# Gate and up of the last feed-forward by seven block products in place of eight, on one Trainium2 core

## The chip, the cores and the metric

The kernel runs on one core of a Trainium2 chip, in one launch. The metric is the device time of one execution in microseconds (us), taken as the median of several executions. The engines go by their names in the profile: PE is TensorE (matrix products), DVE is VectorE, ACT is ScalarE, POOL is GpSimd, and SP is SyncE, which here only issues transfers. SBUF is the on-chip memory, and PSUM is the memory of eight banks into which PE accumulates.

## The reference

The reference is a two-layer block of a diffusion model, in fp32, with 512 latent tokens and 256 context tokens of 1024 features. Each layer mixes tokens in four ways, projects the mixed features (`w_out`), adds the residual, and runs a modulated SwiGLU feed-forward of inner width 2816. In the last layer only the latent tokens are needed. What matters here, cut from it:

```
def rms_norm(x, g):
    return x * lax.rsqrt(jnp.mean(x * x, axis=-1, keepdims=True) + NORM_EPS) * g

def swiglu(h, wg, wu, wd):
    return (jax.nn.silu(h @ wg) * (h @ wu)) @ wd

...
        x = x + g1 * (mix @ w_out[l])
        h = rms_norm(x, g_ffn[l]) * (1 + sc2) + sh2
        x = x + g2 * swiglu(h, w_gate[l], w_up[l], w_down[l])
```

## The kernel before

Features lie on the 128 partitions and tokens along the free axis, so x is eight tiles (`x`, one for each 128 features) of 128 x tokens. Every fp32 product is made of three matmuls (`mm3`, L63): operands are split into a high part in the reduced type fp32r and a rest, and PE multiplies high by high (L65), high by low (L66) and low by high (L67). Weights come in pieces of 128 x 512 (256 KB): SP loads one into a tile `raw` (`load_raw`, L69), ACT copies the high part into a tile `w` (L82), and DVE subtracts it to get the low part (L83). Layer 0 also lets POOL do a few of these.

The end of the last layer, where the change lies, has four stages:

1. Output projection: for each of eight tiles `mt`, 24 matmuls of 512 columns (`proj_out`). DVE adds the residual (L925, in `residual`), ACT squares x (L282) and DVE adds the squares up (L283, both in `Squares.add`), and ACT and DVE make the scaled and split tile `st` for the feed-forward (L253, L254, in `scaled`). The shift of the modulation rides along as two extra token columns.
2. Norm: four one-column matmuls sum the squares over the partitions (L292), DVE makes the reciprocal root (L100 to L109), four matmuls spread it over the partitions (L302), and ACT copies it (L304). The products gate and up need none of it: it is multiplied in afterwards.
3. Gate and up: for each of 22 column tiles `ft` of 128 features, 4 weight pieces and 2 x 2 x 8 groups of three matmuls of 256 or 258 columns. Each of the four results has a PSUM bank. DVE multiplies by the norm (L968, L970), ACT takes the Silu (L969), DVE multiplies the two (L971), and ACT and DVE split the result into a tile `h` (L92, L93).
4. Down: the 22 tiles are taken in three blocks of 8, 7 and 7 (`BLOCKS`). After each, eight output tiles are made from the block's `h` tiles with 512-column matmuls, and added to x.

Tiles share buffers by tag: `BUFS` gives eight to `h` and `st`, six to `w`, three each to `raw`, `T`, `pts` and `row`, two to `mraw`, four to `post`. A tile whose buffers are all in use waits until the oldest has been read for the last time. The order of the instructions on each engine is set when the program is built: a scheduler works it out from its own estimates of when each would be ready. On the chip each engine then goes through its list in that order, and SP through its loads, waiting where it must.

Of the kernel before, what the change touches and what calls it, by code (L numbers as in the profile page):

```python
# [9 lines left out]
F32R = mybir.dt.float32r  # L10
I32 = mybir.dt.int32
AF = mybir.ActivationFunctionType
OP = mybir.AluOpType
# [4 lines left out]
KT = 8  # L18
SEQ = 512
CTX = 256  # L20
NT = SEQ + CTX
DEPTH = 2
FFT = 22
BLOCKS = ((0, 8), (8, 15), (15, 22))
ORDER = (4, 6, 5, 7, 0, 2, 3, 1)

START = "s0 x1 x0 s1 w0 x2 x3 s2 x4 x5 s3 x6 x7 w1 s4 s5 s6 s7"
# [12 lines left out]
def hybrid_block(ctx: ExitStack, tc, t, out):  # L40
    nc = tc.nc
    V, S, G, T = nc.vector, nc.scalar, nc.gpsimd, nc.tensor
# [20 lines left out]
    def mm3(ps, ah, al, bh, bl, start, stop):  # L63

        T.matmul(ps, ah, bh, start=start, stop=False)  # L65
        T.matmul(ps, ah, bl, start=False, stop=False)  # L66
        T.matmul(ps, al, bh, start=False, stop=stop)  # L67
# [180 lines left out]
    def scaled(x, gain, sh, segs):  # L248

        hk = tile("st", [128, 2, NT + 2], F32R)  # L250
        for s0, s1, v in segs:
            hi, lo = [hk[:, z, s0 + 2 * v:s1 + 2 * v] for z in range(2)]
            last_s = S.activation(hi, x[:, s0:s1], AF.Copy, scale=gain[:, v:v + 1])  # L253
            last_v = V.scalar_tensor_tensor(lo, x[:, s0:s1], gain[:, v:v + 1], hi.bitcast(F32),  # L254
                                            op0=OP.mult, op1=OP.subtract)
        split_to(hk[:, 0, SEQ:SEQ + 2], hk[:, 1, SEQ:SEQ + 2], sh)
        made.append((last_s.ins, last_v.ins))
        return hk

    def scaled_proj(w, h, cuts, pss, k):  # L260
        for (c0, c1, *_), ps in zip(cuts[0], pss):
            mm3(ps[:, :c1 - c0], wf(w, k, 0), wf(w, k, 1), h[:, 0, c0:c1], h[:, 1, c0:c1], k == 0, k == KT - 1)

    def shift_of(cuts, pss):
        sh = small.tile([128, 2], F32, tag="sh", name="sh")
# [120 lines left out]
    for l in range(DEPTH):  # L386
        last = l == DEPTH - 1
        segs = segs_lat if last else segs_all
        ntok = segs[-1][1]
        m, a = mods[l]["m"], mods[l]["a"]  # L390
# [8 lines left out]
        first = [("win_c", 0), ("win_c", 1), ("win_dv", 0)]  # L399
        if l == 0:  # L400
# [3 lines left out]
            for what, k in START.split():  # L404
                k = int(k)
# [14 lines left out]
                if what + str(k) == "s5":  # L420
                    r = norm_spread(rr, segs_all, ("md", "md"))
            first = ws
            mods.append(new_mod(1))
        else:
            r = norm_spread(norm_scale(sq, segs_all), segs_all, ("tq", "md"))
            first = [feat_units(*x) for x in first]
# [16 lines left out]
        w = feat_units("win_dv", 1, "mraw")  # L443
# [487 lines left out]
        for mt in range(KT):  # L931
            w = wsplit(t["wout"][l, mt])
            outs = proj_out(w, KT, mh, ORDER, [[["pj", "pj", "tq", "md", "sc", "sc", "pt", "po"], ["pj", "pj", "tq", "md", "sc", "sc", "pt", "po"]][l][(mt * len(segs) + i) % 8] for i in range(len(segs))])
            x = xs[mt]
            residual(x, outs, per_feature(m, 2, mt))
            sq.add(x)
            sh = per_feature(m, 3, mt)
            h.append(scaled(x, a[:, 1, mt], sh[:, 0:1].to_broadcast([128, 2]) if last else sh, segs))

        turn[0] = 0  # L940
        r = norm_spread(norm_scale(sq, segs), segs, ("po", "pt"))
# [12 lines left out]
        work = steps()  # L954
        for b0, b1 in BLOCKS:
            hid = []
            for ft in range(b0, b1):
                gu = [wsplit(t["wg"][l, ft]), wsplit(t["wu"][l, ft])]
                gps, ups = [[psum_any() for _ in range(2)] for _ in range(2)]
                for w, pss in zip(gu, (gps, ups)):  # L960
                    for k in range(KT):
                        scaled_proj(w, h[k], cuts, pss, k)
                shg, shu = shift_of(cuts, gps), shift_of(cuts, ups)
                hd = tile("h", [128, 2, NT], F32R)
                for (_, _, s0, s1, v, o), g_, u_ in zip(cuts[0], gps, ups):
                    n = s1 - s0
                    sg, up = tile("post", [128, 512])[:, :n], tile("post", [128, 512])[:, :n]
                    V.tensor_mul(sg, g_[:, o:o + n], r[:, s0:s1])  # L968
                    S.activation(sg, sg, AF.Silu, bias=shg[:, v:v + 1])  # L969
                    V.tensor_mul(up, u_[:, o:o + n], r[:, s0:s1])  # L970
                    V.scalar_tensor_tensor(up, up, shu[:, v:v + 1], sg, op0=OP.add, op1=OP.mult)  # L971
                    split_to(hd[:, 0, s0:s1], hd[:, 1, s0:s1], up)
                for _ in range(3):
                    next(work, None)
# [62 lines left out]
def _layouts(i):  # L1037
    ac = np.ascontiguousarray
    L = DEPTH
    o = {}  # L1040
    xt = np.concatenate([i["x"][0].T, i["ctx"][0].T], 1)
    o["xt"] = ac(xt.reshape(KT, 128, NT).transpose(1, 0, 2))
    o["cc"] = ac(np.stack([i["c"][0], i["c_ctx"]], 1).reshape(KT, 128, 2).transpose(1, 0, 2))
    cols = []
    for u in range(2):
        cols += [np.arange(512) + 512 * u, np.arange(512) + 1024 + 512 * u]
    cols += [np.arange(2048, 6144)]
    cols = np.concatenate(cols)
# [24 lines left out]

    def featmajor(x, k):
        n = x.shape[2] // 128
        x = x.reshape(L, k, 128, n, 128).transpose(0, 3, 2, 1, 4)
        return ac(x)

    o["win_c"] = featmajor(i["w_in"][:, :, 1024:1280], KT).reshape(L, 2, 128, 1024)
    o["win_dv"] = featmajor(i["w_in"][:, :, 1792:2048], KT).reshape(L, 2, 128, 1024)  # L1080
    wo = np.concatenate([i["w_out"][:, swap], i["w_out"][:, 256:]], 1)
    o["wout"] = featmajor(wo, KT).reshape(L, KT, 128, 1024)
    o["wg"] = featmajor(i["w_gate"], KT).reshape(L, FFT, 128, 1024)
    o["wu"] = featmajor(i["w_up"], KT).reshape(L, FFT, 128, 1024)
    o["wd"] = featmajor(i["w_down"], FFT)
    for n in ("a_q_gain", "a_k_gain", "d_q_gain", "d_k_gain", "a_sink", "b_v_gain"):
        o[n] = ac(i[n])
    o["ws"] = ac(i["b_w_s"].transpose(0, 3, 1, 2).reshape(L, 128, 512))
    o["bs"] = ac(i["b_b_s"].transpose(0, 2, 1))

    o["wpool"] = ac(i["c_w_pool"].reshape(L, 2, 2, 64, 64).transpose(0, 2, 3, 1, 4))
    o["csc"] = ac(i["c_scale"].reshape(L, 2, 128).transpose(0, 2, 1))

    p = np.pad(i["d_rpb"], ((0, 0), (0, 0), (0, 0), (8, 9)))
    r, cq, kr, x = np.ogrid[:8, :16, :8, :32]
    o["rpb"] = ac(p[:, :, kr - r + 7, x - 8 - cq + 15 + 8].reshape(L, 4, 128, 8, 32))
    return o
# [17 lines left out]
```

## Time and profile before

| | |
|---|---|
| median of 3 runs | 1545.6 us (1543.95 to 1546.96) |
| the profiled execution | 1543.86 us |
| its span in the trace | 1542.1 us |
| mean granted TensorE clock in the span | 0.996 of full speed |
| PE busy | 1508.3 us (98%) |
| DVE busy | 956.9 us (62%) |
| ACT busy | 618.8 us (40%) |
| POOL busy | 118.3 us (8%) |

The span is the time from the first to the last instruction that the profile records; the execution's own time holds another 1.8 us. Busy time of an engine is the time in which at least one of its instructions runs. A matmul's recorded duration is longer than its share of PE's time, since matmuls overlap: what a matmul costs is the distance from its start to the start of the next.

### The profile page before, as it was taken

To read this page: it belongs to the slowest core of one execution; us is meant where nothing else is said; L and a number is where in the kernel's file an instruction comes from. 1 tells how busy PE (TensorE), PEld (TensorE's weight loads), DVE (VectorE), ACT (ScalarE), POOL (GpSimd) and SP (SyncE) were. 2 spreads that over 40 slices of the span, in tenths; PEclk is the share of its full clock that TensorE was granted. 3 is DMA by queue.
4 is the path that set the end of the run, shared out by engine and by line. 5 is a ranking of instruction groups with operands and counts; after the bars stand their busy time and mean duration, and the time that the engine had idled before them with its cause. 6 is when DMAs were issued, how large, how long until landed. Compare 5 with 4: busy or idle time off the path is not lost.

```text
span 1542.1 us, 26166 instructions
## 1 busy us (share of the span) xinstructions
PE 1508.3 (98%) x10098; PEld 1330.2 (86%) x10098; DVE 956.9 (62%) x2317; ACT 618.8 (40%) x1278; POOL 118.3 (8%) x107
## 2 busy tenths in 40 slices
PE   6899999999999999999999999899999999999999
PEld 4788787788888888888888888889889998998997
DVE  3789877686485624843375458899865443544453
ACT  5547655643322112221222344477654332332331
POOL 2521200100000000000000004542000000000000
PEclk9999999999999999999999999999999999999999
DMA  8443223342243313722273232201232233233223
GB/s 313 128 144 102 93 80 108 126 141 76 89 144 111 122 62 101 234 62 63 82 230 96 71 105 76 83 32 44 89 101 90 93 94 98 90 88 105 89 86 100
DMA packets 79324, 163.39 MB, mean 106 GB/s; under 512 B 12000, under 2 KB 17760, under 8 KB 79200
## 3 DMA queue, kind: packets, MB, share of 16 engines
q1 hardware_dynamic: 79200, 161.73, 32.8%
q8 instruction: 79, 1.29, 0.3%
q14 instruction: 45, 0.37, 0.1%
HBM read 157.50 MB, written 4.19 MB: 105 GB/s over the span
## 4 chain that ended last, share of the span: by engine, by line
PE 87%; DVE 6%; DMA 4%; ACT 2%; issue 1%; POOL 1%; SPq 0%; ACTq 0%; POOLq 0%
PE pj L65 9%; PE pj L66 9%; PE pj L67 9%; PE sc L66 6%; PE sc L65 6%; PE sc L67 6%; PE tq L65 3%; PE tq L66 3%; PE tq L67 3%; PE po L66 3%; PE po L65 3%; PE po L67 3%; PE po L350 2%; PE pt L66 2%; PE pt L65 2%; PE pt L67 2%
## 5 line engine op out<-in xcount | busy, mean ns | idle before, releaser
L82 ACT ACTIVATE w<-raw 128x512 fp32r<-128x512 f32 x368 | 227.1, 621 | 617.6 <-PE sc L67 154.2
L83 DVE TENSOR_TENSOR w<-raw,w 128x512 fp32r<-128x512 f32 x336 | 226.7, 677 | 242.9 <-ACT w L82 242.6
L65 PE MATMUL pj<-w,h 128*128 128x256 f32 x480 | 138.4, 289 | 6.7 <-DVE post L499 5.9
L66 PE MATMUL pj<-w,h 128*128 128x256 f32 x480 | 138.7, 289 | 0.0
L67 PE MATMUL pj<-w,h 128*128 128x256 f32 x480 | 137.7, 287 | 0.0
L65 PE MATMUL pj<-st,w 128*128 128x258 f32 (+2 forms) x384 | 120.4, 314 | 2.5 <-ACT st L253 2.3
L66 PE MATMUL pj<-st,w 128*128 128x258 f32 (+2 forms) x384 | 120.0, 313 | 0.0
L66 PE MATMUL sc<-st,w 128*128 128x258 f32 (+2 forms) x384 | 119.8, 312 | 0.0
L65 PE MATMUL sc<-st,w 128*128 128x258 f32 (+2 forms) x384 | 119.7, 312 | 0.0
L67 PE MATMUL pj<-st,w 128*128 128x258 f32 (+2 forms) x384 | 119.5, 312 | 0.0
L67 PE MATMUL sc<-st,w 128*128 128x258 f32 (+2 forms) x384 | 118.9, 310 | 0.0
L65 PEld LDWEIGHTS pj<-w,h 128*128 128x128 f32 x480 | 92.1, 192 | 13.9 <-ACT post L494 5.5
L83 POOL TENSOR_TENSOR w<-raw,w 128x512 fp32r<-128x512 f32 x32 | 43.0, 1354 | 739.0 <-DVE row L283 633.3
L66 PEld LDWEIGHTS pj<-w,h 128*128 128x128 f32 x480 | 92.4, 192 | 1.7 <-DVE post L499 0.8
L67 PEld LDWEIGHTS pj<-w,h 128*128 128x128 f32 x480 | 92.3, 192 | 0.3 <-issue 0.2
L65 PEld LDWEIGHTS pj<-st,w 128*128 128x128 f32 x384 | 73.1, 190 | 9.5 <-ACT st L253 3.5
L67 PEld LDWEIGHTS pj<-st,w 128*128 128x128 f32 x384 | 72.6, 189 | 5.5 <-issue 1.7
L65 PEld LDWEIGHTS sc<-st,w 128*128 128x128 f32 x384 | 73.2, 191 | 4.5
L66 PEld LDWEIGHTS pj<-st,w 128*128 128x128 f32 x384 | 72.7, 189 | 4.8 <-issue 0.4
L66 PEld LDWEIGHTS sc<-st,w 128*128 128x128 f32 x384 | 72.7, 189 | 4.2
L67 PEld LDWEIGHTS sc<-st,w 128*128 128x128 f32 x384 | 72.3, 189 | 4.0
L65 PE MATMUL po<-st,w 128*128 128x512 f32 (+1 forms) x192 | 66.2, 345 | 0.0
(308 smaller groups left out, 4117.9 us busy)
## 6 DMA issues: line engine op xcount, KB each, us to landing
mraw<-in_wmod SPq DMA_DIRECT2D x80, 512.0 KB, 3.9
raw<-in_wg SPq DMA_DIRECT2D x88, 256.0 KB, 2.5
raw<-in_wu SPq DMA_DIRECT2D x88, 256.0 KB, 2.6
raw<-in_wd SPq DMA_DIRECT2D x64, 256.0 KB, 2.7
h<-in_wslab SPq DMA_DIRECT2D x16, 512.0 KB, 8.1
raw<-in_wout SPq DMA_DIRECT2D x32, 256.0 KB, 2.6
x<-in_xt SPq DMA_DIRECT2D x16, 384.0 KB, 5.4
raw<-in_wd SPq DMA_DIRECT2D x32, 192.0 KB, 2.4
```

The lines of the kernel that those rows point to most:

```text
L65: T.matmul(ps, ah, bh, start=start, stop=False)
L66: T.matmul(ps, ah, bl, start=False, stop=False)
L67: T.matmul(ps, al, bh, start=False, stop=stop)
L82: S.activation(w[:, 0, :n], raw, AF.Copy)
L83: eng.tensor_sub(w[:, 1, :n], raw, w[:, 0, :n].bitcast(F32))
L350: T.matmul(o[64 * hh:64 * hh + 64, :128], vs[hh][lo:hi], pts[i, hh], start=i == 0, stop=i == n - 1)
```

## The change

In the last layer, gate and up are no longer made tile by tile. Two column tiles (`ft`, `ft + 1`) and the two halves of the tokens form a 2 x 2 block product over the two halves of the features (even and odd tiles of 128), and this is made from seven block products in place of eight (`strassen`). Each has 4 x 3 matmuls of 258 columns, and its operands are sums of blocks:

- `token_blocks` and `token_forms` make the seven token operands once for the whole stage, from each two tiles of x, in place of `scaled`: four blocks in a tile `mraw`, four sums in another (L291 to L294), and the split parts of all seven in the tiles `f1`, `f2`, `f3` (tags `T`, `bias` and `st`).
- `weight_forms` makes the seven weight operands of each pair and each of gate and up. Three are blocks of the weights as they are, two of them loaded as one tile `mraw` of 512 KB. The other four are sums, made by transfers: SP loads one block, and then POOL issues a second transfer that adds to it (`accum_op`, L313). Two of the sums, `s2` and `s4`, add a sum that was made before. All seven are then split as before, by ACT and DVE.
- The seven results in PSUM are put together by DVE (L347 to L356) and ACT (L346) into tiles `post`, and norm, Silu and the product of gate and up run over 512 tokens at a time.
- The blocks of the feed-forward are of 8, 8 and 6 column tiles in place of 8, 7 and 7, in both layers, and the weights of gate and up lie in another column order, which layer 0 follows by taking its slices in another order (`at`).

The diff, cut to its core:

```diff
-BLOCKS = ((0, 8), (8, 15), (15, 22))
+BLOCKS = ((0, 8), (8, 16), (16, 22))
...
+    def token_blocks(par, x, gain, sh, b):
+
+        S.activation(by128(b[:, 2 * par:2 * par + 2, 0:HN]), halves(x), AF.Copy, scale=gain[:, 0:1])
+        for h in (2 * par, 2 * par + 1):
+            V.tensor_copy(b[:, h, HN:HN + 2], sh[:, 0:1].to_broadcast([128, 2]))
+
+    def token_forms(b, single):
+
+        u = tile("mraw", [128, 4, HN + 2])
+        V.tensor_sub(u[:, 1], b[:, 0], b[:, 1])
+        V.scalar_tensor_tensor(u[:, 2], u[:, 1], -1.0, b[:, 3], op0=OP.mult, op1=OP.subtract)
+        V.tensor_add(u[:, 0], b[:, 2], u[:, 2])
+        V.tensor_sub(u[:, 3], b[:, 3], b[:, 1])
+        f1 = tile(single, [128, 1, 2, HN + 2], F32R)
+        f2 = tile("st", [128, 3, 2, HN + 2], F32R)
+        f3 = tile("st", [128, 3, 2, HN + 2], F32R)
+        for f, i, src in ((f2, 0, b[:, 2:4]), (f1, 0, b[:, 0:1]), (f3, 0, u[:, 1:4]), (f2, 2, u[:, 0:1])):
+            n = src.shape[1]
+            split_to(f[:, i:i + n, 0], f[:, i:i + n, 1], src)
...
+    def weight_forms(src):
+
+        both = load_raw(src[0], "mraw")
+        a11, a12 = both[:, 0:512], both[:, 512:1024]
+        a22 = load_raw(src[1][:, 512:1024], "raw", 512)
+
+        def plus(tag, first, more):
+
+            z = load_raw(first, tag, 512)
+            G.dma_start(z, more, accum_op=OP.add)
+            return z
...
+        s1 = plus("pts", src[1][:, 0:512], src[1][:, 512:1024])
+        s3 = plus("raw", src[0][:, 0:512], src[1][:, 0:512])
+        s2 = plus("pts", src[0][:, 0:512], s1)
+        s4 = plus("row", src[0][:, 512:1024], s2)
+        yield parts(a12)
+        yield parts(a11)
+        for x in (s1, s2, s4, a22, s3):
+            yield parts(x)
...
+        c1, c2 = tile("post", [128, 2, n]), tile("post", [128, 2, n])
+        u = tile("br", [128, n])
+        p2, p1 = product(2), product(1)
+        S.activation(u, p1, AF.Copy)
+        V.tensor_add(c1[:, 0], p2, u)
+        p5, p6 = product(5), product(6)
+        V.tensor_add(u, p6, u)
+        V.tensor_add(c1[:, 1], p5, u)
+        p3 = product(3)
+        V.tensor_add(c1[:, 1], p3, c1[:, 1])
+        p4, p7 = product(4), product(7)
+        V.tensor_add(c2[:, 0], p7, u)
+        V.scalar_tensor_tensor(c2[:, 1], p5, -1.0, c2[:, 0], op0=OP.mult, op1=OP.subtract)
+        V.tensor_sub(c2[:, 0], p4, c2[:, 0])
+        return c1, c2
...
+            for ft in range(b0, b1, 2) if last else ():
+                rv = halves(r)
+                gate = strassen([t["wg"][l, ft], t["wg"][l, ft + 1]], h)
+                for c in gate:
+                    cv = c[:, :, 0:HN]
+                    V.tensor_mul(by128(cv), by128(cv), rv)
+                    S.activation(cv, cv, AF.Silu, bias=c[:, 0, HN:HN + 1])
+                up = strassen([t["wu"][l, ft], t["wu"][l, ft + 1]], h)
+                for c, g_ in zip(up, gate):
+                    cv = c[:, :, 0:HN]
+                    V.tensor_mul(by128(cv), by128(cv), rv)
+                    V.scalar_tensor_tensor(cv, cv, c[:, 0, HN:HN + 1], g_[:, :, 0:HN], op0=OP.add, op1=OP.mult)
+                    hd = tile("h", [128, 2, NT], F32R)
+                    split_to(halves(hd[:, 0]), halves(hd[:, 1]), by128(cv))
+                    hid.append(hd)
```

The order of instructions moves in two places of which the prediction speaks. The first is on PE, where the last layer's output projection ends. The names are the results and operands: `po<-h,w` is the last output tile, `pj<-st,w` a gate product, `tq<-ones,row` the sum of squares and `po<-ident,ry` the spread of the norm. Before, the end of the projection is followed at once by gate products:

```order
L66 MATMUL po<-h,w 128x512
L67 MATMUL po<-h,w 128x512
L65 MATMUL pj<-st,w 128x256
L66 MATMUL pj<-st,w 128x256
L67 MATMUL pj<-st,w 128x256
L65 MATMUL pj<-st,w 128x258
```

and the sum of squares follows 41 gate matmuls after the last L67 of the projection:

```order
L65 MATMUL pj<-st,w 128x258
L66 MATMUL pj<-st,w 128x258
L292 MATMUL tq<-ones,row 128x1 x4
L67 MATMUL pj<-st,w 128x258
```

In the changed kernel the same place on PE reads so (L387 is what was L292, and L397 what was L302):

```order
L66 MATMUL po<-h,w 128x512
L67 MATMUL po<-h,w 128x512
L387 MATMUL tq<-ones,row 128x1 x4
L397 MATMUL po<-ident,ry 128x128 x4
L65 MATMUL pj<-st,w 128x258
L66 MATMUL pj<-st,w 128x258
L65 MATMUL pj<-T,w 128x258
L66 MATMUL pj<-T,w 128x258
```

The sum of squares and the spread of the norm now stand between the projection and the first product, with no other matmul beside them.

The second place is SP's list of loads from the last weights of the output projection (`in_wout`) on. Before, pieces of gate (`in_wg`) and up (`in_wu`) follow in turn, each into a `raw` tile:

```order
L72 DMA raw<-in_wout 128x512 x4
L72 DMA raw<-in_wg 128x512 x2
L72 DMA raw<-in_wu 128x512 x2
L72 DMA raw<-in_wg 128x512 x2
L72 DMA raw<-in_wu 128x512 x2
```

In the changed kernel (two loads into `pts` stand ahead of the last weights of the projection):

```order
L72 DMA raw<-in_wout 128x512 x4
L72 DMA raw<-in_wg 128x512 x2
L72 DMA raw<-in_wu 128x512
L72 DMA mraw<-in_wg 128x1024
L72 DMA mraw<-in_wu 128x1024
L72 DMA mraw<-in_wg 128x1024
L72 DMA row<-in_wg 128x512
L72 DMA pts<-in_wu 128x512
L72 DMA row<-in_wu 128x512
```

The tile `mraw` with the first two weight operands stands behind everything that held the two `mraw` buffers before, and the first load into `row` behind the third load into `mraw`. With it POOL, which had nothing to do in this stage, gets a list of transfers that add up. It starts so, with the tiles' numbers in the program: 12485 and 12491 are `s1` and `s2` of the first gate pair, 12488 its `s3`, 12494 its `s4`, and 12628, 12634 and 12637 are `s1`, `s2` and `s4` of the first up pair.

```order
L313 DMA pts_12485<-in_wg 128x512
L313 DMA pts_12491<-pts_12485 128x512
L313 DMA pts_12628<-in_wu 128x512
L313 DMA raw_12488<-in_wg 128x512
L313 DMA row_12494<-pts_12491 128x512
L313 DMA pts_12634<-pts_12628 128x512
L313 DMA row_12637<-pts_12634 128x512
L313 DMA pts_12777<-in_wg 128x512
```

A sum of sums (`pts_12491<-pts_12485`, then `row_12494<-pts_12491`) waits for the one before it to land, and all that stands below it waits with it.

## Rows read from the trace of the kernel before

**Rows 1.** The page's first part: busy time, share of the span and instructions of each engine.

```profile
PE 1508.3 (98%) x10098; PEld 1330.2 (86%) x10098; DVE 956.9 (62%) x2317; ACT 618.8 (40%) x1278; POOL 118.3 (8%) x107
```

**Rows 2.** Windows: length; busy PE, PEld, DVE, ACT, POOL; clock; DMA share; GB/s.

```profile
1164.00:1540.00 376.00, 374.30 (x2658) 353.18 (x2657) 177.36 (x388) 120.45 (x223) 0.00 (x0) 1.00 0.30 93
1180.00:1237.00 57.00, 57.00 (x479) 57.00 (x478) 30.25 (x72) 21.69 (x43) 0.00 (x0) 1.00 0.29 93
```

**Rows 3.** All waits of PE, 1100 to 1543 us: what for, total us, times, longest.

```profile
PE pj L65 <- ACT h L92: 0.3, 1, 0.3
```

**Rows 4.** Timeline of PE, end of the projection and norm: start, duration, line, shape.

```profile
1164.05 0.39 PE L67 MATMUL po<-h,w 128*128 128x512 f32 x1
1164.28 0.28 PE L65 MATMUL pj<-st,w 128*128 128x256 f32 x1
...
1169.17 0.95 PE L292 MATMUL tq<-ones,row 128*128 128x1 f32 x8
...
1175.44 1.06 PE L302 MATMUL po<-ident,ry 128*128 128x128 f32 x8
```

**Rows 5.** Timeline of ACT at the same place, and a pair of 512-column operations.

```profile
1165.33 0.63 ACT L282 ACTIVATE row<-x 128x512 f32<-128x512 f32 x1 [0.21 <-DVE x L925]
1165.86 0.71 ACT L253 ACTIVATE st<-x,a 128x512 fp32r<-128x512 f32 x1
...
1189.18 0.63 ACT L82 ACTIVATE w<-raw 128x512 fp32r<-128x512 f32 x1 [2.23 <-PE md L67]
1189.72 0.49 ACT L969 ACTIVATE post<-post,sh 128x256 f32<-128x256 f32 x1
```

**Rows 6.** Timeline of DVE: operations that follow each other without a wait, and the norm.

```profile
1103.29 0.68 DVE L83 TENSOR_TENSOR w<-raw,w 128x512 fp32r<-128x512 f32 x1
1103.89 0.68 DVE L755 SCALAR_TENSOR_TENSOR post<-post,pj 128x512 f32<-128x512 f32 x1
...
1142.73 0.75 DVE L254 SCALAR_TENSOR_TENSOR st<-x,a,st 128x512 fp32r<-128x512 f32 x1
1143.39 0.16 DVE L93 TENSOR_TENSOR st<-mod,st 128x2 fp32r<-128x2 f32 x1
...
1164.48 0.75 DVE L925 SCALAR_TENSOR_TENSOR x<-po,mod,x 128x512 f32<-128x512 f32 x1 [1.36 <-PE po L67]
...
1165.99 0.69 DVE L283 TENSOR_TENSOR row<-row 128x512 f32<-128x512 f32 x1 [0.15 <-ACT row L282]
1170.16 0.16 DVE L100 TENSOR_SCALAR rx<-tq 128x4 f32<-128x4 f32 x1 [1.45 <-PE tq L292]
...
1172.77 0.16 DVE L109 SCALAR_TENSOR_TENSOR ry<-rz,ry 128x4 f32<-128x4 f32 x1
...
1177.22 0.42 DVE L968 TENSOR_TENSOR post<-pj,row 128x256 f32<-128x256 f32 x1 [1.85 <-ACT row L304]
1177.56 0.41 DVE L970 TENSOR_TENSOR post<-sc,row 128x256 f32<-128x256 f32 x1
```

**Rows 7.** Transfers by issue: name, queue, count, size, median us to landing.

```profile
mraw<-in_wmod SPq DMA_DIRECT2D x80, 512.0 KB, 3.9
raw<-in_wg SPq DMA_DIRECT2D x88, 256.0 KB, 2.5
```

**Rows 8.** Busy time by window early on, columns as in rows 2, transfers at their densest.

```profile
20.00:25.00 5.00, 4.50 (x38) 2.89 (x40) 0.06 (x1) 2.07 (x3) 4.12 (x3) 1.00 1.03 406
```

**Rows 9.** Timeline of PE early on, after a wait of over 1 us.

```profile
55.58 0.80 PE L65 MATMUL tq<-st,mraw 128*128 128x512 f32 x1 [1.10 <-DVE red L206]
```

**Rows 10.** Windows of 1 us around it, columns as in rows 2.

```profile
55.00:56.00 1.00, 0.42 (x1) 0.42 (x2) 1.00 (x3) 0.55 (x2) 0.00 (x0) 0.81 0.37 137
56.00:57.00 1.00, 1.00 (x3) 0.75 (x3) 1.00 (x5) 0.63 (x2) 0.00 (x0) 0.50 0.72 245
...
58.00:59.00 1.00, 1.00 (x6) 0.91 (x5) 1.00 (x3) 1.00 (x3) 1.00 (x2) 0.50 0.36 135
59.00:60.00 1.00, 1.00 (x7) 0.88 (x6) 1.00 (x3) 1.00 (x3) 1.00 (x1) 0.99 0.77 217
```

More of the change, by code (lines that the diff above doesn't have):

```diff
@@ L258, in scaled, with scaled_proj, halves @@
         return hk
-    def scaled_proj(w, h, cuts, pss, k):
+    def scaled_proj(w, h, cuts, pss, k, at=None):
+        at = k if at is None else at
         for (c0, c1, *_), ps in zip(cuts[0], pss):
-            mm3(ps[:, :c1 - c0], wf(w, k, 0), wf(w, k, 1), h[:, 0, c0:c1], h[:, 1, c0:c1], k == 0, k == KT - 1)
+            mm3(ps[:, :c1 - c0], wf(w, at, 0), wf(w, at, 1), h[:, 0, c0:c1], h[:, 1, c0:c1], k == 0, k == KT - 1)
+    HN = SEQ // 2
+    def halves(x):
+        return x[:, :SEQ].rearrange("p (c h t) -> p h c t", h=2, t=128)
@@ new lines, in by128 @@
+    def by128(x):
+        return x.rearrange("p h (c t) -> p h c t", t=128)
+    def token_blocks(par, x, gain, sh, b):
[14 more added lines that the diff above has]
+            split_to(f[:, i:i + n, 0], f[:, i:i + n, 1], src)
+        at = {1: (f1, 0), 2: (f2, 0), 3: (f2, 1), 4: (f2, 2), 5: (f3, 0), 6: (f3, 1), 7: (f3, 2)}
+        return {p: (f[:, i, 0], f[:, i, 1]) for p, (f, i) in at.items()}
@@ new lines, in weight_forms, with parts @@
+    def weight_forms(src):
[6 more added lines that the diff above has]
+            return z
+        def parts(x):
+            w = tile("w", [128, 2, 512], F32R)
+            split_to(w[:, 0], w[:, 1], x)
+            return w
+        s1 = plus("pts", src[1][:, 0:512], src[1][:, 512:1024])
[6 more added lines that the diff above has]
+            yield parts(x)
@@ new lines, in strassen, with product @@
+    def strassen(src, forms):
+        wfs = weight_forms(src)
+        n = HN + 2
+        def product(p):
+            ps = psum_any()[:, :n]
+            w = next(wfs)
+            for kk, f in enumerate(forms):
+                mm3(ps, w[:, 0, 128 * kk:128 * kk + 128], w[:, 1, 128 * kk:128 * kk + 128], *f[p],
+                    kk == 0, kk == len(forms) - 1)
+            return ps
+        c1, c2 = tile("post", [128, 2, n]), tile("post", [128, 2, n])
[13 more added lines that the diff above has]
+        return c1, c2
@@ L937, in hybrid_block @@
             sh = per_feature(m, 3, mt)
-            h.append(scaled(x, a[:, 1, mt], sh[:, 0:1].to_broadcast([128, 2]) if last else sh, segs))
+            if not last:
+                h.append(scaled(x, a[:, 1, mt], sh, segs))
+                continue
+            if mt % 2 == 0:
+                blocks = tile("mraw", [128, 4, HN + 2])
+            token_blocks(mt % 2, x, a[:, 1, mt], sh, blocks)
+            if mt % 2:
+                h.append(token_forms(blocks, "T" if mt < 6 else "bias"))
         turn[0] = 0
@@ L956, in hybrid_block @@
             hid = []
-            for ft in range(b0, b1):
+            for ft in range(b0, b1, 2) if last else ():
[13 more added lines that the diff above has]
+                    hid.append(hd)
+            for ft in () if last else range(b0, b1):
                 gu = [wsplit(t["wg"][l, ft]), wsplit(t["wu"][l, ft])]
@@ L961, in hybrid_block @@
                     for k in range(KT):
-                        scaled_proj(w, h[k], cuts, pss, k)
+                        scaled_proj(w, h[k], cuts, pss, k, 4 * (k % 2) + k // 2)
                 shg, shu = shift_of(cuts, gps), shift_of(cuts, ups)
@@ L1082, in _layouts @@
     o["wout"] = featmajor(wo, KT).reshape(L, KT, 128, 1024)
-    o["wg"] = featmajor(i["w_gate"], KT).reshape(L, FFT, 128, 1024)
-    o["wu"] = featmajor(i["w_up"], KT).reshape(L, FFT, 128, 1024)
+    o["wg"], o["wu"] = [ac(featmajor(i[n], KT).reshape(L, FFT, 128, 4, 2, 128).transpose(0, 1, 2, 4, 3, 5))
+                        .reshape(L, FFT, 128, 1024) for n in ("w_gate", "w_up")]
     o["wd"] = featmajor(i["w_down"], FFT)
```

## The prediction

> **What bounds the kernel now.** I read the page's first part first, then windows of the stage that changes, then the waits of PE, and last the timelines at the two ends of the stage. PE is busy 98% of the span [rows 1], and from 1164 us to 1540 us, which is the last layer's feed-forward, it is busy 374.30 of 376.00 us while DVE needs 177.36, ACT 120.45, POOL nothing, and the transfers 0.30 of the engines' time [rows 2]. In that whole stage PE's only recorded wait is 0.3 us [rows 3]. So the stage costs what its matmuls cost, and two other engines and the transfers have room. Removing matmuls must pay in full, unless the operands that replace them come late.
>
> **What is removed.** Before, gate and up take 22 x 2 x 2 x 8 x 3 = 2112 matmuls of 256 or 258 columns; now 11 pairs x 2 x 7 products x 4 x 3 = 1848, all of 258. In a stretch of nothing else, 479 matmuls fill 57.00 us [rows 2]: 0.119 us each. The 264 fewer save **31.4 us**. A product is 1.43 us, one `strassen` (seven) 10.0 us, a pair of column tiles 20.0 us. The down projection keeps its count.
>
> **The start of the stage.** Before, the first gate product started 0.23 us after the last projection matmul [rows 4], because its weights and the `st` tiles but the last, which ACT began at 1165.86 [rows 5], were there; sum of squares and spread came later, under cover. Now no product stands ahead of them in PE's list, and the first weight operand can't be loaded until the token operands are done: both `mraw` buffers hold the last token blocks and sums. Take 1164.28 as zero. The residual ends at +0.95 [rows 6], Square at +1.7 [rows 5], the addition of squares at +2.4 [rows 6], and the sum over partitions takes 0.95 more [rows 4]: +3.4. On DVE three sums of 258 columns (about 1.05 from the 0.34 between the two 256-column rows of [rows 6] and 0.06 for the one with a scalar) and the split of two blocks (0.6) end at about +4.2, which frees the first `mraw`. Its 512 KB land 3.9 us later [rows 7], ACT copies in 0.6 [rows 5]: the first product can start at about +8.9, and its low part follows with some 0.2 of waiting. The other branch, the split of three sums (0.9), one of 258 (0.3) and the root's chain, 2.6 + 0.16 long before [rows 6], ends at +7.3, its spread (1.06, [rows 4]) at +8.3, and so lies beneath. PE stands at +9.1 where before it had 9.1 us of work, 2.0 of it the same norm matmuls [rows 4]: **+7.1 us**. If the load can start 2 us sooner the spread ends last, and it is 6; with 1 us more on each of three hand-overs it is 10.
>
> PE has idled then for several microseconds. After a wait of 1.10 us [rows 9], with others shortly before, the granted clock was 0.50 from about 55.8 to 59.0 us and full again after it [rows 10]: 3.2 us at 1.2 in place of 2.4 GHz lose 1.6. I take the same here: **+1.6 us** (0 to 4).
>
> **The first sum of sums.** Let L be the time from the issue of an adding transfer to its landing. No row shows one. Below it is bounded by a plain 256 KB, 2.5 us, above by three plain ones in turn, 7.5; the nearest row is that of 512 KB, 3.9 [rows 7], if an addition moves both what is there and what is added. I take L = 4. In the first pair `s4` goes into a `row` tile whose load stands in SP's list behind a third `mraw` load, which waits for the first split. That split ends near +10.4; the load lands 3.4 later (behind 512 KB on the same engines), the addition at +17.8, the split (0.54 and 0.60) at +19.0. PE wants it for the fifth product, at 9.1 + 4 x 1.43 + 1.6 = +16.4: **+2.5 us** (1 at L = 2.5, 6 at 7.5).
>
> **In steady state** three loops must each fit. DVE does per pair 14 weight splits at 0.60, 12 operations of 258 columns from PSUM at 0.34, 2 with a scalar at 0.40, 4 products of 512 at 0.60, 2 with a scalar at 0.66, 2 splits of 512 at 0.60 (distances between starts in [rows 6]): 8.4 + 4.1 + 0.8 + 2.4 + 1.3 + 1.2 = 18.2 us of PE's 20.0. ACT does 14 copies, 2 of 258, 2 Silu and 2 more of 512, at 0.54 [rows 5] about 10.5. The transfers are 7 loads of 256 KB for each `strassen`, at 406 GB/s, where the engines are full [rows 8], 0.65 us each, and four that add: 7.1 us of 10.0 if an addition costs what a copy does, 9.7 if it costs two. The third loop is the chain of sums. The `pts` tile of `s2` is the one of the previous `s1`: split of `s1`, load of `s2` (2.5), two additions (2L), copy and split of `s4` (1.1), 3.6 + 2L, and from the third product of one to the fifth of the next there are nine products, 12.9 us. It fits while L is below 4.6; at 4 it takes 11.6. The order is fixed at build time and DVE is at 91%, so some products will wait for a split or an eviction. I put 0.3 us on a pair (0 to 1): **+3 us** (0 to 11).
>
> **At nothing:** between blocks PE must wait some 5 us for the last `h` tiles, but for each output tile the first 18 of 24 matmuls of 512 columns (0.23 each, [rows 4]) don't need them, 4.1 us a tile, and several tiles have a bank; without that cover it would be 15 us for three blocks. Layer 0's other slice order and block lengths move no work: the same matmuls from the same six `w` buffers. The wider block of 8 in place of 7 makes the weight pieces 256 KB, and the transfers of the down stage are as far from full as before.
>
> **Sum:** -31.4 + 7.1 + 1.6 + 2.5 + 3 = -17.2 us. On the profiled execution (1543.9) that is 1526.7; the median of the runs is 1.7 above it, so **1528.5, said 1529 us**.
>
> The Trainium skill ("DMA: Bandwidth & Descriptors", Anatomy of one DMA, the GpSimd path) fits a transfer of that path with 2.0 us plus bytes over 436 GB/s, which for 256 KB is an estimate of 2.6 us; by it the first sum of sums would cost 1 and not 2.5, the total 1527, and the chain loop would have 4 us to spare. No row here shows a transfer of that path that adds.
>
> **Rivals.**
>
> *The chain of sums is too long.* If L is above 4.6, nine products take 3.6 + 2L: each us of L costs 2 x 7/9 = 1.56 us for each of 22 `strassen`, 34 us in all, less about 7 us at the start of each of the two later blocks, where the down stage lets five splits run ahead. The gain is gone at L = 5.5, and at L = 6 it is 34 x 1.4 - 14 = +34: about **1562**. For it speaks that the chain at L = 4 already takes 90% of its time, that POOL issues in order, so every addition behind a waiting one waits too, and that these transfers share engines that would be two to three times as busy as now. Against it, 512 KB land in 3.9 [rows 7] and half the time of a small transfer is no data at all (0.65 of 2.5).
>
> *The transfer engines are full.* If an addition costs three copies, a `strassen` needs 4.5 + 4 x 1.95 = 12.3 us of them against 10.0: 2.3 x 22 = 50, less 14: about **1565**. At two copies it is 9.7 and still fits, but with hardly a gap, and landings grow later. The Trainium skill ("Collectives: The Full Stack", The bandwidth ceiling) states that a reduction moves at half the rate of a copy, since each add needs two source reads; by that rule it is the 9.7, and the sum stays as it is. No row here shows an adding transfer, so its price is open.
>
> *DVE is the bound.* At 18.2 of 20.0 with evictions that PE's banks wait for, each us of a pair beyond 20 costs 11 us. Waits in DVE's list, for ACT's copies or for `post` tiles, of 1.8 us in a pair use up the slack; at 3.8 us a pair takes 22, which is +22 in place of the +3 above: about **1547**, no change. Against it, DVE has slack again in every down stage.
>
> **Chances.** Forecast's case (PE bound, a gap at the start) 0.56, chain 0.20, full transfer engines 0.12, DVE 0.12. The forecast's case alone runs from 1522 (no steady waits, a short L, no clock loss) to 1541 (all upper ends but the gap). The whole range begins 2 us below that, 1520, for a start gap that is shorter than I think, and ends at 1566, which takes in the two slow rivals as worked out above and leaves out a longer L (at 7.5 it would be 1528.5 + 34 x 2.9 - 14 = 1613) and what is worse than three copies. A change of under 0.2%, 3 us, is about what a measurement of this kernel can't tell from none. Faster: nearly all of the first case (0.54), some of DVE's (0.05), few of the others (0.04). Same: 0.02 of the first, 0.04 of DVE's, 0.03 where L is near 5.5. Slower: the rest, 0.28.
>
> **What would show it.** In the changed trace: 264 fewer matmuls of 258 at an unchanged 0.12 us; a hole of 7 to 9 us on PE after the last `po<-h,w`, ended by the load of `mraw`, and a clock of 0.5 for some 3 us behind it; a wait of PE in the first `strassen` at the fifth product, with the `row` transfer as what is late; DVE busy some 90% and transfers 0.7 to 1.0 between 1180 and 1500 us; adding transfers that land in about 4 us; and no wait above 0.5 us per pair. The prediction is wrong if these transfers take 5 us or more, which would show as waits for splits of `row` in every `strassen` with DVE idle at the same time, or if PE waits for evictions, with DVE at 99%.

## The result: 2.2% slower, and the profile after

The changed kernel takes 1579.3 us (median of 4 runs, 1576.4 to 1585.6) against 1545.0: the ratio is 1.022, with an interval of 1.020 to 1.025. 1529 was forecast, with 1566 as the upper end. The profiled execution took 1576.39 us, with a span of 1574.6.

The page's first part, to be held against [rows 1]:

```profile
PE 1504.6 (96%) x9834; PEld 1316.5 (84%) x9834; DVE 1036.3 (66%) x2437; ACT 657.8 (42%) x1330; POOL 195.0 (12%) x195
```

The 264 matmuls are gone (9834 against 10098), yet the span grew by 32.5 us. So about 64 us of something else came in. The windows of the feed-forward and of a stretch of products in it, columns as in rows 2, say what kind it is:

```profile
1164.00:1571.00 407.00, 372.61 (x2392) 342.12 (x2392) 256.43 (x485) 153.61 (x274) 72.95 (x84) 0.95 0.74 183
1182.00:1280.00 98.00, 86.80 (x620) 84.65 (x620) 67.67 (x132) 41.98 (x76) 25.54 (x30) 0.88 0.91 220
```

Against [rows 2], PE has 34 us in which nothing runs, its clock is 0.95 where it was 1.00, and the transfers have gone from 0.30 to 0.74 of the engines' time, 0.91 in the stretch of products. DVE is busy 69% there, so DVE isn't what PE lacks. The waits of PE from 1150 to 1580 us, where [rows 3] had one of 0.3 us (what for, total us, times, longest):

```profile
PE pj L65 <- ACT w L92: 9.0, 4, 3.7
PE pj L65 <- DVE post L355: 4.5, 3, 2.3
PE tq L65 <- ACT w L92: 4.2, 1, 4.2
PE po L397 <- DVE ry L109: 3.4, 1, 3.4
PE sc L65 <- ACT w L92: 2.9, 1, 2.9
PE po L65 <- ACT w L92: 2.8, 2, 2.4
PE md L65 <- DVE post L355: 2.5, 2, 1.5
PE tq L387 <- DVE row L378: 2.2, 1, 2.2
```

Two waits are those of the norm at the start, 5.6 us. The rest are for splits of weight operands (L92) and for the eviction that frees a bank (L355). The chain of work that ended last, cut to 1200 to 1240 us (start, length, what), shows what stands behind both:

```profile
1199.38 7.14 DMA pts<-in_wu
...
1207.10 5.31 DMA pts<-pts
...
1212.69 7.03 DMA row<-pts
...
1219.82 0.64 ACT w L92
...
1227.08 7.24 DMA pts<-in_wu
...
1234.89 4.64 DMA pts<-pts
...
1239.82 5.09 DMA row<-pts
```

A load of 256 KB takes 7.1 us, the addition to `s2` 5.3, the addition to `s4` 7.0, one after another, and only then comes the split. The chain is made of transfers almost alone. What each queue took of the engines (packets, MB, share of sixteen engines' span; q1 is SP's queue, q0 POOL's), and how long transfers take by kind from issue to landing (columns as in rows 7):

```profile
q1 hardware_dynamic: 85536, 179.04, 35.7%
q0 software_dynamic: 12672, 23.07, 8.5%
pts<-in_wu SPq DMA_DIRECT2D x22, 256.0 KB, 4.5
row<-in_wg SPq DMA_DIRECT2D x11, 256.0 KB, 3.5
pts<-pts POOLq DMA_DIRECT2D x22, 256.0 KB, 4.5
mraw<-in_wg SPq DMA_DIRECT2D x11, 512.0 KB, 5.6
row<-pts POOLq DMA_DIRECT2D x22, 256.0 KB, 6.4
pts<-in_wg POOLq DMA_DIRECT2D x11, 256.0 KB, 6.3
```

Even plain loads have become slow: 3.5 to 4.7 us for the pieces of 256 KB, by kind from 1164 us on, and 5.6 for 512, against 2.5 and 3.9 in [rows 7]. 88 additions of 256 KB took 8.5% of sixteen engines' 1574.6 us, which is 134 us or 1.52 each, where the densest stretch of before moved a plain 256 KB in 0.65 [rows 8].

Where the 64 us lie can be added up from PE's timeline: the distance from each row to the next, less 0.119 or 0.227 us for its width, sorted by whether the next row names a wait, and whether the granted clock stands at 0.50 there. What is left over is spread over some 2200 matmuls.

| from 1164 us on, us | at waits | at the half clock | spread |
|---|---|---|---|
| before | 0 | 0 | 1 |
| changed | 38 | 18 | 8 |

So 18 of these 64 us are no wait: behind several of the longer waits the granted clock is at its lower level, 1.2 GHz, for some microseconds. The window 1200 to 1220, which holds one wait of 2.9 us up to 1207.13, has a mean clock of 0.83, with 0.50 from 1207 to 1213:

```profile
1200.00:1220.00 20.00, 17.09 (x119) 16.83 (x118) 10.93 (x21) 5.46 (x11) 4.32 (x5) 0.83 0.88 213
...
1205.00:1206.00 1.00, 0.00 (x0) 0.00 (x0) 0.00 (x0) 0.00 (x0) 0.00 (x0) 1.00 0.58 164
...
1207.00:1208.00 1.00, 0.87 (x3) 0.86 (x4) 0.90 (x2) 1.00 (x3) 0.86 (x1) 0.50 0.44 158
...
1212.00:1213.00 1.00, 1.00 (x6) 1.00 (x6) 0.73 (x2) 0.49 (x1) 0.31 (x1) 0.50 0.84 211
```

### The profile page after: what moved, and what is told of

It reads as the page before. It is cut to its first block, busy times and chain, and to the rows that moved or that the text cites. A ratio compares the mean times of both kernels' runs of the same rounds, so it can differ in the third digit from the quotient of the medians.

```text
span 1574.6 us, 26176 instructions
## 1 busy us (share of the span) xinstructions
PE 1504.6 (96%) x9834; PEld 1316.5 (84%) x9834; DVE 1036.3 (66%) x2437; ACT 657.8 (42%) x1330; POOL 195.0 (12%) x195
## 4 chain that ended last, share of the span: by engine, by line
PE 71%; DMA 13%; DVE 8%; issue 3%; ACT 2%; POOL 1%; SPq 0%; POOLq 0%; ACTq 0%; DVEq 0%
PE pj L65 7%; PE pj L66 7%; PE pj L67 7%; PE sc L66 5%; PE sc L65 5%; PE sc L67 5%; DMA row<-pts 4%; PE tq L66 3%; PE tq L67 3%; PE tq L65 3%; PE po L67 3%; PE po L66 3%; PE po L65 3%; PE po L445 2%; DMA pts<-in_wu 2%
## 5 line engine op out<-in xcount | busy, mean ns | idle before, releaser
L82 ACT ACTIVATE w<-raw 128x512 fp32r<-128x512 f32 (+1 forms) x280 | 171.2, 617 | 430.2 <-PE md L67 95.4
L83 DVE TENSOR_TENSOR w<-raw,w 128x512 fp32r<-128x512 f32 x248 | 164.5, 668 | 76.8 <-ACT w L82 76.6
L67 PE MATMUL pj<-w,h 128*128 128x256 f32 x480 | 136.4, 284 | 0.0
L65 PE MATMUL pj<-st,w 128*128 128x512 f32 (+2 forms) x344 | 112.3, 326 | 15.4 <-ACT w L92 9.0
L65 PE MATMUL sc<-st,w 128*128 128x512 f32 (+2 forms) x344 | 111.4, 324 | 2.9 <-ACT w L92 2.9
L66 PE MATMUL pj<-st,w 128*128 128x512 f32 (+2 forms) x344 | 111.0, 323 | 0.8 <-DVE st L254 0.8
L66 PE MATMUL sc<-st,w 128*128 128x512 f32 (+2 forms) x344 | 111.0, 323 | 0.0
L67 PE MATMUL pj<-st,w 128*128 128x512 f32 (+2 forms) x344 | 110.0, 320 | 0.4 <-DVE w L93 0.4
L67 PE MATMUL sc<-st,w 128*128 128x512 f32 (+2 forms) x344 | 109.8, 320 | 0.0
L65 PEld LDWEIGHTS pj<-w,h 128*128 128x128 f32 x480 | 90.9, 190 | 14.3 <-ACT post L589 5.5
L66 PEld LDWEIGHTS pj<-w,h 128*128 128x128 f32 x480 | 91.2, 190 | 1.7 <-DVE post L594 0.8
L67 PEld LDWEIGHTS pj<-w,h 128*128 128x128 f32 x480 | 91.2, 190 | 0.3 <-issue 0.2
L65 PEld LDWEIGHTS pj<-st,w 128*128 128x128 f32 x344 | 67.3, 196 | 24.7 <-ACT w L92 12.3
L65 PEld LDWEIGHTS sc<-st,w 128*128 128x128 f32 x344 | 68.1, 198 | 7.6 <-ACT w L92 3.1
L66 PEld LDWEIGHTS pj<-st,w 128*128 128x128 f32 x344 | 67.2, 195 | 5.6 <-DVE st L254 1.0
L67 PEld LDWEIGHTS pj<-st,w 128*128 128x128 f32 x344 | 67.3, 196 | 4.8 <-DVE w L93 0.9
L66 PEld LDWEIGHTS sc<-st,w 128*128 128x128 f32 x344 | 67.8, 197 | 4.1
L67 PEld LDWEIGHTS sc<-st,w 128*128 128x128 f32 x344 | 67.4, 197 | 4.1
L65 PE MATMUL pj<-h,w 128*128 128x512 f32 (+1 forms) x180 | 63.9, 363 | 0.8 <-ACT h L92 0.7
```

The lines of the kernel that those rows point to most:

```text
L82: S.activation(w[:, 0, :n], raw, AF.Copy)
L83: eng.tensor_sub(w[:, 1, :n], raw, w[:, 0, :n].bitcast(F32))
```

## The experiments

Theory A is the chain of sums: waits in turn, held in a loop by the buffer that `s2` shares with the previous `s1`. Theory B is full transfer engines. Theory C is that the lists of DVE and ACT hold PE whatever the transfers do. All windows below are 1182 to 1280 us.

**Without the additions** (`no_adds`):

```diff
             z = load_raw(first, tag, 512)
-            G.dma_start(z, more, accum_op=OP.add)
             return z
```

> All four adding transfers are left out (the sums are then single blocks); the seven loads, their order on SP, the splits and the products stay. Theories A and B both: 1520 to 1535 us, transfer share near 0.5 and PE waiting only at the start of the stage. A third theory, C, that DVE's and ACT's lists hold PE whatever the transfers do: above 1550 us.

1523.9 us, ratio 0.986 (0.984 to 0.988).

```profile
1182.00:1280.00 98.00, 98.00 (x707) 92.68 (x706) 80.56 (x151) 49.50 (x83) 0.00 (x0) 1.00 0.57 170
```

PE doesn't stop once in this stretch, with DVE at 82% and all splits and evictions in place. C falls; the additions cost 55 us. Its sums at waits, at the half clock and spread are 4, 2 and 6 us.

**Other sources, no sum of sums** (`no_chain`):

```diff
-        s2 = plus("pts", src[0][:, 0:512], s1)
-        s4 = plus("row", src[0][:, 512:1024], s2)
+        s2 = plus("pts", src[0][:, 0:512], src[1][:, 0:512])
+        s4 = plus("row", src[0][:, 512:1024], src[1][:, 512:1024])
```

> s2 and s4 add a weight block where they added a sum (so the sums are not those of the method); loads, their order on SP, and the number and size of the adding transfers stay. Theory A, the chain of sums: in the changed kernel the s2 load waits for the split of the previous s1 (5.7 us to land at 1212.76), then two additions in turn (7.5 and 8.2 us) stand before the split of s4; without the chain PE's waits for splits of row go, with the waits for evictions and the low clock behind them: 1528 to 1545 us. Theory B, full transfer engines: they have as much to move, their share stays above 0.85 in the blocks, and additions still take 5 us or more: 1565 to 1580 us.

1572.1 us, ratio 1.017 (1.016 to 1.019), 7 us less than the changed kernel, in the range of theory B:

```profile
1182.00:1280.00 98.00, 87.72 (x641) 85.38 (x642) 67.79 (x131) 42.19 (x77) 26.50 (x31) 0.91 0.95 227
```

The engines' share is 0.95, and additions to `row` land in 7.2 to 7.9 us. That one sum waits for another is worth little here. It isn't a clean test: the two sums now add from memory, which takes longer to land than from SBUF (5.0 against 3.4 us in `add_alone` below), and `s2` still waits for its buffer. (The landings of 5.7, 7.5 and 8.2 us in the expectation are not those of the trace shown above, which has 7.1, 5.3 and 7.0.)

**Another buffer for `s2`** (`wide_chain`): the whole computation.

```diff
-                h.append(token_forms(blocks, "T" if mt < 6 else "bias"))
+                h.append(token_forms(blocks, "T" if mt < 6 else "wph"))
...
-        s2 = plus("pts", src[0][:, 0:512], s1)
+        s2 = plus("bias", src[0][:, 0:512], s1)
```

> The whole computation, with the sums chained as in the changed kernel, but s2 in two buffers of its own (tag bias; the token operand that lay there goes to wph), so its load no longer waits for the split of the previous s1. Theory A in its narrow form, the loop is closed by that buffer: 1530 to 1550 us. Theory B, full transfer engines: within 6 us of the changed kernel, 1573 to 1585 us, as the same bytes move.

1552.9 us, ratio 1.0045 (1.003 to 1.006): 26 us less, between the two forecasts. The same bytes move by the same chain of sums, but the loads of `s2` may start earlier. The scheduler used that: two of them stand ahead of the last projection weights, and some of POOL's additions change places, so the 26 us belong to the buffer and the new order together:

```profile
1182.00:1280.00 98.00, 89.09 (x657) 85.02 (x657) 70.78 (x139) 44.42 (x81) 26.13 (x30) 0.97 0.99 238
```

Now the engines are busy 0.99 of the time, and bring 238 GB/s where plain transfers brought 406 [rows 8]. So the buffer's loop is real, but it is about half of the loss, and the other half, 29 us above the kernel without additions, stands with full engines in this window.

**The price of an addition by itself** (`add_alone`, `plain_alone`): the kernel before with transfers beside it, for each column tile; in the second without `accum_op`.

```diff
+                if last:
+                    za = load_raw(t["wg"][l, ft][:, 0:512], "pts", 512)
+                    G.dma_start(za, t["wg"][l, ft][:, 512:1024], accum_op=OP.add)
+                    zb = load_raw(t["wu"][l, ft][:, 0:512], "pts", 512)
+                    G.dma_start(zb, za, accum_op=OP.add)
```

> The kernel before, with four transfers a column tile beside it that nothing waits for, into tiles not used: a load of 256 KB and an addition from memory to it, another load and an addition of the first sum to it, in the last layer's gate and up. It measures an addition at a third to a half of the transfer engines' time. In the changed kernel an addition took 1.52 us of all sixteen engines (8.5% of 1574.6 us for 88), 2.3 plain pieces. If that is its own price: 44 additions take 67 us of engine time and land in 3 to 4 us. If it was the crowding that made them dear: nearer 44 x 0.65 = 29 us, landing in 2.5 to 3. The time of the whole: within 5 us of the kernel before.

> The same with the two additions made plain copies on the same POOL queue (leaves the sums out; nothing uses them). If the adding is what costs: 44 copies take about 29 us of engine time and land in some 2.5 us. If POOL's queue is what costs: as much as the additions.

One run each: 1598.7 and 1567.9 us. The expectation for the whole time missed, since SP issues in order and stood at these tiles' loads (113 us in waits for `pts<-pts` in the first kernel) with the weights behind them. The price came out. First the additions, then the copies:

```profile
q0 software_dynamic: 6336, 11.54, 4.5%
pts<-in_wg POOLq DMA_DIRECT2D x22, 256.0 KB, 5.0
pts<-pts POOLq DMA_DIRECT2D x22, 256.0 KB, 3.4
```

```profile
q0 software_dynamic: 3520, 11.54, 2.2%
pts<-in_wg POOLq DMA_DIRECT2D x22, 256.0 KB, 3.3
pts<-pts POOLq DMA_DIRECT2D x22, 256.0 KB, 3.1
```

44 additions took 4.5% of 1596.9 us, 72 us or 1.63 each; 44 copies of the same bytes on the same queue 2.2% of 1566.1, 34.5 us or 0.78 each. An addition is 144 packets where a copy is 80, and costs 2.1 times a copy, with the engines 0.50 busy from 1164 to 1560 us (0.44 with the copies). It lands in 3.4 us from SBUF and 5.0 from memory.

**Copies in place of the additions, and short additions** (`plain_copies`, `short_adds`). In the first the list of every engine is, row for row, that of the changed kernel:

```diff
-            G.dma_start(z, more, accum_op=OP.add)
+            G.dma_start(z, more)
```

```diff
-            G.dma_start(z, more, accum_op=OP.add)
+            G.dma_start(z[:, 0:64], more[:, 0:64], accum_op=OP.add)
```

> The changed kernel with each adding transfer made a plain copy of the same bytes on the same queue (the additions are left out); SP's and POOL's lists are the same, row for row, so the chain of waits and the buffers are too. If the price of adding fills the engines (1.63 us against 0.78 in the two measurements by themselves): 7 x 0.65 + 4 x 0.78 = 7.7 of 10.0 us, landings near 3.5 us, 1526 to 1538 us. If the chain of waits through one queue holds by itself: 1555 us or more.

> The changed kernel with each addition over 64 of its 512 columns (the other columns' sums are left out): the same chain of waits in the same order, an eighth of the bytes. If the landing of an addition is mostly a fixed time, of 4.5 us or more, the chain still holds PE: 1545 to 1570 us. If it is the moving of the bytes, in crowded engines: landings of 2 to 3 us, a chain of about 9 of its 12.9 us, 1522 to 1530 us.

1541.0 us, ratio 0.997 (0.996 to 0.998), and 1531.5, ratio 0.991 (0.989 to 0.992). In the window:

```profile
1182.00:1280.00 98.00, 92.82 (x676) 88.57 (x676) 74.35 (x144) 45.20 (x80) 15.32 (x29) 0.96 0.74 241
```

```profile
1182.00:1280.00 98.00, 96.67 (x707) 92.27 (x707) 80.08 (x154) 48.89 (x87) 26.15 (x30) 0.98 0.68 182
```

Both missed their range, by 3.0 and 1.5 us, on the side of the chain. With the same lists and buffers, and the same bytes handed over, 38 us of the changed kernel go away when nothing is added. The remaining 17 above the kernel without additions I put down to the chain with landings of 3.4 to 5.0 us; that is argued, as the engines are also busier than there (0.74 against 0.57). With an eighth of the bytes an addition still lands in 3.2 to 4.0 us, with the engines at 0.68, so most of a landing of 3.4 to 5.0 us does not shrink with the bytes. That kernel is 8 us above the one without additions.

**The sums on POOL** (`pool_sums`, whole computation): blocks are loaded once, and POOL adds them in SBUF.

```diff
+        a21 = load_raw(src[1][:, 0:512], "raw", 512)
...
-            z = load_raw(first, tag, 512)
-            G.dma_start(z, more, accum_op=OP.add)
+            z = tile(tag, [128, 512])
+            G.tensor_add(z, first, more)
...
-        s4 = plus("row", src[0][:, 512:1024], s2)
+        s4 = plus("row", a12, s2)
```

> The whole computation; the four sums made by POOL from blocks in SBUF (two loads of 256 KB and one of 512 KB a strassen in place of seven pieces and four additions). A and B both: 1520 to 1537 us, transfer share near 0.3, POOL at 4 x 1.35 = 5.4 of 10 us by the POOL subtractions of the profile. C, or a DVE slowed beside a busy POOL: above 1545 us with DVE over 90% busy.

1561.5 us, ratio 1.010 (1.009 to 1.012): the rival came true.

```profile
1182.00:1280.00 98.00, 87.84 (x638) 84.14 (x637) 94.05 (x143) 43.10 (x77) 34.11 (x25) 0.95 0.32 95
```

The engines are free, and DVE is at 96%, with fewer instructions than in the kernel without additions. POOL's timeline and then DVE's at one place:

```profile
1209.09 1.29 POOL L314 TENSOR_TENSOR pts<-mraw,pts 128x512 f32<-128x512 f32 x1 [2.88 <-issue]
```

```profile
1208.28 0.68 DVE L93 TENSOR_TENSOR w<-pts,w 128x512 fp32r<-128x512 f32 x1
1208.88 0.42 DVE L351 TENSOR_TENSOR post<-pj,br 128x258 f32<-128x258 f32 x1
1209.21 1.72 DVE L93 TENSOR_TENSOR h<-post,h 128x512 fp32r<-128x512 f32 x1
1210.86 0.68 DVE L93 TENSOR_TENSOR w<-pts,w 128x512 fp32r<-128x512 f32 x1
```

The DVE operation that runs beside POOL's addition takes 1.72 us, its like before and after it 0.68. Over the whole stage the 66 such splits of 512 columns (L93) that overlap a POOL addition by 0.4 us or more take 1.46 us in the median, the 110 that overlap none 0.68. Of PE's 28 us of waits 17 are now for evictions by DVE (L356 in this kernel). Four additions a `strassen` thus take the bound from the transfers to DVE.

**Some of the sums on POOL** (`pool_s4`, then `pool_s24`, whole computation): `wide_chain` with `s4`, or `s2` and `s4`, added by POOL from SBUF (`pool_sum` is a `tensor_add` on POOL as above).

```diff
-        s4 = plus("row", src[0][:, 512:1024], s2)
+        s4 = pool_sum("row", a12, s2)
```

> The whole computation: s2 in buffers of its own, s1, s2 and s3 by adding transfers, s4 by POOL from SBUF. The transfers of a strassen fall from 7 x 0.65 + 4 x 1.52 = 10.6 us of all engines to 6 x 0.65 + 3 x 1.52 = 8.5, of 10.0. One POOL addition a strassen slows DVE's work beside it by 0.7 us or so, to about 9.8. If full engines were what was left in the kernel with wider buffers: 1524 to 1540 us. If DVE now holds: 1540 to 1550, with DVE over 93% and waits for evictions.

> The whole computation: as the last one (s2 and s4 on POOL, s1 and s3 by adding transfers) without the 23 matmuls in the gap. If those only lengthened the gap, as the kernel with s4 alone on POOL suggests (1546.0 with them, 1540.4 without): 1535 to 1540 us. If they cost nothing and the difference lay elsewhere: 1541 to 1546 us.

1540.4 us, ratio 0.9966 (0.9952 to 0.9979), and 1540.1, ratio 0.9963 (0.9951 to 0.9976). Both are faster than the kernel before, by a third of a percent. The first and the second:

```profile
1182.00:1280.00 98.00, 92.14 (x674) 86.71 (x674) 78.81 (x143) 44.81 (x80) 30.10 (x29) 1.00 0.81 200
```

```profile
1182.00:1280.00 98.00, 89.94 (x663) 85.81 (x662) 90.53 (x143) 43.93 (x79) 33.06 (x30) 0.98 0.61 159
```

In the first the engines are at 0.81 and DVE at 80%; waits, half clock and spread are down to 14, 2 and 8 us. With `s2` on POOL as well the engines fall to 0.61 and DVE rises to 92%, and the time stays: what one side gives, the other takes.

**Matmuls in the gap at the start** (`pool_s4_warm`, `pool_s24_warm`): 23 matmuls of 512 columns that nothing reads, meant to hold the clock.

```diff
+        def warm(n):
+            ps = psum("sc")
+            for i in range(n):
+                T.matmul(ps[:, :512], wf(w, 7, 0), mh[7][:, 0, 0:512], start=i == 0, stop=i == n - 1)
+
+        if last:
+            warm(9)
+        r = norm_scale(sq, segs)
+        if last:
+            warm(14)
+        r = norm_spread(r, segs, ("po", "pt"))
```

> The whole computation: as the kernel with s4 on POOL, and 23 matmuls of 512 columns into a bank that nothing reads stand in the gap between the output projection and the first product (5.2 us). If the low clock behind the gap is a cost (0.81 over 18 us of window, 3.4 us): 3 to 5 us faster than 1540.4. If the clock falls for another reason, or the gap gets longer by them: within 1 us of it, or slower.

> The whole computation: s2 and s4 on POOL, s1 and s3 by adding transfers, with the 23 matmuls in the gap. Engines: 5 x 0.65 + 2 x 1.6 = 6.5 of 10.0 us. If full engines are still the larger cost with s4 alone on POOL: 1525 to 1533 us. If DVE beside a busy POOL is: 1536 to 1548 us, with DVE over 90% in the blocks.

1546.0 us, ratio 1.000 (0.999 to 1.001), and 1543.3, ratio 0.998 (0.997 to 1.000): worse than without them by 6 us in the first pair, and by 3 in the second, where the intervals of the two ratios overlap. All 23 were placed ahead of the sum of squares, PE still stood idle for 2 to 3 us behind them and the sum, and in the first kernel the granted clock was 0.50 from 1172 to 1175 us all the same. Whether a gap that is filled to its end keeps the clock was therefore not tested. Nor was the time lost in the gap. In the profiled executions, from the end of the projection to the first product took 9.2 us against 8.6 in the first pair, and 8.7 against 8.6 in the second. What followed the first product took 7.5 and 4.1 us longer, and why is open.

## Why the prediction was wrong

**The step that failed** is the second of the three loops in the steady state: "7.1 us of 10.0 if an addition costs what a copy does, 9.7 if it costs two", from which it was taken that the transfers fit. An addition by itself costs 1.63 us of all engines, 2.1 copies of its own queue and 2.5 of the 0.65 that I had for a copy. With that the same sum is 7 x 0.65 + 4 x 1.63 = 11.1 us for a `strassen` of 10.0. I had tied the rival of full engines to a price of three copies, 1.95 us, and put 0.12 on it; it needed no more than 1.37, at which 4.55 + 4 x 1.37 is 10.0. In the sum it is the two terms that hang on the additions, 2.5 us for the first `s4` and 3 in steady state, that came out far too small: the additions cost 55.

**The loss is both slow rivals at once.** I had worked them out apart, as 1562 and 1565, and each by itself would have lain in the range. Full engines make every landing longer, and the chain is made of landings. My loop had 2.5 us for the load of `s2` and L = 4 for each addition, 11.6 of 12.9. The value for L was about right in engines half free (3.4 from SBUF in `add_alone`, 5.0 from memory). In full ones the chain above took 7.1 + 5.3 + 7.0 us, and by the medians of the changed kernel the loop is 4.5 + 4.5 + 6.4 and 1.1 for the split, 16.5 of 12.9. Additions of 5 us or more with DVE idle were the prediction's own sign of being wrong. It came: five of the six kinds land in 5.4 to 6.5 us, and PE waits 19 us for splits with DVE at 69%, though not in every `strassen`. Loosening the loop (`wide_chain`) gave back 26 us, removing only the adding (`plain_copies`) 38, and removing the four transfers 55; the parts overlap, so they can't be added. That the adding makes 38 of them is shown, with every list unchanged; how the rest divides between the chain and the crowd is not.

**What the waits cost twice.** The steady term, 3 us, had no clock in it. Of the changed kernel's 64 us, 18 are at the half clock. I had counted 1.6 us for it, once, at the start.

**What held.** 264 matmuls fewer, at 0.120 us in the kernel without additions (500 in 60.00 us from 1190 to 1250), against 0.119: the saving is about 30 us. The down projection kept its count but not its price: its 528 matmuls of 512 columns are 0.233 us apart in the median, in the changed kernel and without additions, against 0.227 before, which is 3 us; why is open. The start of the stage was 8.55 us against 9.1: the projection's last matmul starts at 1161.76 and takes 0.23, the first product starts at 1170.54. Rows of PE, and one of ACT:

```profile
1161.76 0.39 PE L67 MATMUL po<-h,w 128*128 128x512 f32 x1
1164.38 1.05 PE L387 MATMUL tq<-ones,row 128*128 128x1 f32 x8 [2.23 <-DVE row L378]
1168.81 2.07 PE L397 MATMUL po<-ident,ry 128*128 128x128 f32 x8 [3.38 <-DVE ry L109]
1170.54 0.56 PE L65 MATMUL pj<-st,w 128*128 128x258 f32 x1
...
1181.57 0.39 PE L65 MATMUL tq<-st,w 128*128 128x258 f32 x1 [4.24 <-ACT w L92]
```

```profile
1169.55 1.15 ACT L92 ACTIVATE w<-mraw 128x512 fp32r<-128x512 f32 x2 [3.35 <-DMA mraw<-in_wg]
```

The spread of the norm and the first weights (the first of ACT's two copies) came out almost together there. The first `s4` was late by 4.24 us, at the fifth product, where 2.5 was forecast. DVE at 82% and PE without a wait (`no_adds`) show that DVE's list was no bound, as forecast. The ends of the blocks cost nothing: PE waited 0.7 us for `h` tiles in all. That kernel's 1523.9 lies close to the 1529 that were forecast for the whole: all but the additions was sized about right, or its errors cancelled (DVE was busy 82% there, where 91% was forecast). Three slips in the prediction's working change none of this. The other branch of the start adds up on DVE to 4.2 + 0.9 + 0.3 + 2.8 = 8.2 and not 7.3. The upper ends of the forecast's case give 1542 and not 1541. And 0.65 of 2.5 us is a quarter, so by that figure three quarters of a small transfer's time, not half, was no data.

The Trainium skill ("Collectives: The Full Stack", The bandwidth ceiling), writing of rings of cores, has a reduction move at half the rate of a copy; 1.63 against 0.78 us agrees with it. I had cited it and concluded that the sum stays as it is, taking the copy at 0.65 us, where a copy of POOL's queue took 0.78. The fit of the Trainium skill ("DMA: Bandwidth & Descriptors", Anatomy of one DMA) gives an estimate of 2.6 us for 256 KB on that path; measured were 3.1 and 3.3 for copies and 3.4 and 5.0 for additions, and 4.5 to 6.5 for additions in the changed kernel.

## What to carry to other kernels

Before replacing matmuls by moved data, add up the transfer engines' time for one period with each transfer at a price measured for its kind, and take a sum near the whole period as no fit. The runs set no limit: with a share of 0.81 from 1182 to 1280 us `pool_s4` was a third of a percent faster than before, with 0.91 to 0.99 three kernels were slower, and the loads of gate and up pieces of 256 KB took, by kind, 3.4 to 4.7 us in the first and 3.5 to 6.6 in the others, against 2.5. A chain of transfers must be costed with landings in the crowd that the change itself makes, and its buffers are the first thing to widen. A wait on PE can also cost the clock behind it, here 18 us on 38 us of waits.

## What was not expected of the hardware

An adding transfer took 2.1 times the engine time of a copy on the same queue (1.63 against 0.78 us for 256 KB), and 144 packets against 80. Additions over 64 columns in place of 512, an eighth of the bytes, still took 3.2 to 4.0 us to land.

A DVE operation on two SBUF operands of 512 columns takes 0.68 us, and 1.72 where a POOL addition of 1.29 us runs beside it (1.46 in the median of 66), about as if it had waited for most of that addition. DVE's sums with one operand from PSUM (L351, L355, L356 in `pool_sums`) kept their 0.41 to 0.43 us beside POOL. The Trainium skill ("SBUF — State Buffer", Who interferes with whom) says that a DVE instruction with two SBUF inputs contends with a GpSimd instruction that reads SBUF; these rows agree, and give its price.
